# The state's part of a Mamba-2 SSD output: head by head into the output's PSUM bank, with a scaled C, in place of one matmul, a scaled copy and transposes

## The chip, the core and the metric

The kernel runs on one core of one Trainium2 chip. The metric is device time in microseconds (us), the median of several executions. The engines are named as the profile names them: PE is TensorE (PEld its weight loads), DVE is VectorE, ACT is ScalarE, POOL is GpSimd, and SP is SyncE, which issues DMAs here. Each engine runs its own instructions strictly in the order in which they stand, and waits for the others by semaphores. POOL also issues some of the DMAs, from the same queue of instructions in which its arithmetic stands.

## The reference

The kernel computes one hybrid decoder layer on 528 tokens (16 meta tokens and 512 real ones, width 1024): a Mamba-2 SSD branch and a forgetting-attention branch, gated and merged. The change is in the SSD branch. It has 32 heads of 64 channels in 4 groups of 8 heads, a state of 128 per channel, and chunks of 128 tokens. What matters of the reference:

```python
xdt = (xh * dt[..., None]).reshape(Bsz, nc, CHUNK, G, R, P)
a_cs = jnp.cumsum(adt, axis=-1)
seg = a_cs[..., :, None] - a_cs[..., None, :]
decay = jnp.exp(jnp.where(causal, seg, -jnp.inf))
cb = jnp.einsum("bclgn,bcsgn->bcgls", cm, bm)
y_diag = jnp.einsum("bcgls,bcgrls,bcsgrp->bclgrp", cb, decay, xdt)
...
def step(h, inp):
    s, d = inp
    return h * d[..., None, None] + s, h
_, h_in = lax.scan(step, h0, (states, chunk_decay))
y_off = jnp.einsum("bclgn,bcgrpn,bcgrl->bclgrp", cm, h_in, jnp.exp(a_cs))
return (y_diag + y_off).reshape(Bsz, Lp, H, P)
```

`y_off` is the state's part: C of a token times the state at the chunk's start, scaled by the decay since then, which differs for each head and token.

## The kernel before

The work is one long list of projections (the helper `gemm`, line 106: 128-wide weight columns against all tokens, in three products of split halves, `uhi`/`ulo` against `whi`/`wlo`) with the two branches' own work between them. The program is written group by group; a scheduler with a timeline of its own then sets the order of the instructions on each engine, so that projections stand between the pieces of the SSD work. A weight tile comes by DMA (`raw`), ACT rounds it (line 90, `whi`) and DVE takes the rest (line 91, `wlo`). A projection's PSUM tile `mm` has 2 buffers, so a projection can start when the one before the last has been copied out (lines 380, 411, 691 on ACT, line 693 on DVE).

The SSD core (`ssd_core`, below) goes over 4 groups, and in a group over 5 chunks: chunk 0 holds the meta tokens, chunks 1 to 4 have 128 tokens each and an output. I call what chunk c from 1 to 4 does for the output block c. For a block before the change:

- A DMA from POOL's queue (line 449) brings the cumulated log decay of 8 heads, repeated over 128 partitions, into `ab`, one of 4 buffers `big`.
- DVE subtracts a column for each head (line 451, 8 instructions, in place), ACT takes the exponential of the tile (line 453), DVE multiplies by the masked C·B (line 454).
- PE transposes the chunk's x into `px` (line 440); DVE scales it to `xdt` (line 443) and `xdd` (line 446). PE makes the chunk's own state from `xdd` (line 466, into `pst`).
- The state's part: PE multiplies C with the state `h` (line 456, tokens on partitions, into `py`), ACT scales each head's 64 columns by its decay (line 460, 8 instructions, into `y`), and PE transposes the four 128-column pieces of `y` into the output's PSUM tile `pt` (line 477).
- The chunk's own part: 8 matmuls of 64 weight columns, one a head, add into `pt` (line 481). The heads of even number write partitions 0 to 63, the others 64 to 127.
- DVE adds `pt` to the skip (line 486). POOL decays the state (line 471) and DVE adds `pst` (line 472); `h` has 2 buffers.

All PSUM tiles but `mm` come from one pool `ax` of 4 banks. Buffers of a name are used in turn, so in the kernel before the transfer of a block takes the buffer of the same block of the group before.

Of the kernel before, what the change touches and what calls it, by code (L numbers as in the profile page):

```python
# [37 lines left out]
def hybrid_kernel(ctx, tc, x, meta, norm_pre, w_in, conv_w, conv_b, dt_bias, a_log, d_skip,  # L38
# [25 lines left out]
    def big4(shape=(P, 1024)):  # L64
        return st("big4", list(shape), BUFS["big4"])
# [4 lines left out]
    def ax_ps():  # L70
        return axp.tile([P, 512], F32, tag="ax", name=nm("ax"))

    V, S, PE, GP = nc.vector, nc.scalar, nc.tensor, nc.gpsimd
    HE, UE, SE, YS_ACT = GP, V, V, True
# [297 lines left out]
    eac = cst.tile([P, 5, 32], F32, name="eac")  # L372
    S.activation(eac, ac_t, AF.Exp)
# [19 lines left out]
    def heads(ap):  # L393
        return ap.rearrange("p (h x) -> p h x", h=HG)
# [21 lines left out]
    def ssd_core(g, bt, ct, xs, zs):  # L416
# [18 lines left out]
        for c in range(5):  # L435
# [11 lines left out]
            if c:  # L447
                ab = big4((P, HG, P))
                nc.gpsimd.dma_start(out=ab, in_=acs_d[hs, a:b].partition_broadcast(P))
                for i in range(HG):  # L450
                    V.tensor_scalar(ab[:, i], ab[:, i], ac_t[:, c, g * HG + i:g * HG + i + 1], 0.0,  # L451
                                    op0=ALU.subtract, op1=ALU.min)
                S.activation(ab, ab, AF.Exp)  # L453
                V.tensor_mul(ab, ab, cbt[:, c - 1].unsqueeze(1).broadcast_to([P, HG, P]))
                py = ax_ps()
                PE.matmul(py, ct[:, a:b], h, start=True, stop=True)  # L456
                y = row("tmp", (P, T))
                if YS_ACT:
                    for i in range(HG):
                        S.activation(y[:, i * 64:(i + 1) * 64], py[:, i * 64:(i + 1) * 64], AF.Copy,  # L460
                                     scale=eac[:, c, g * HG + i:g * HG + i + 1])
                else:
                    V.tensor_mul(heads(y), heads(py), hb(eac[:, c, hs]))
# [10 lines left out]
            if c:  # L474
                pt = ax_ps()
                for j in range(4):
                    PE.matmul(pt[:, j * P:(j + 1) * P], y[:, j * P:(j + 1) * P], ident,  # L477
                              is_transpose=True, start=j == 0, stop=False)
                for i in range(HG):
                    r = (i % 2) * 64  # L480
                    PE.matmul(pt[r:r + 64, (i // 2) * P:(i // 2 + 1) * P],  # L481
                              xdt[:, i * 64:(i + 1) * 64], ab[:, i], start=False,
                              stop=i >= HG - 2)
# [362 lines left out]
```

## Time and profile before

| | before |
|---|---|
| median of 3 runs | 853.15 us (852.42 to 853.45) |
| the profiled execution | 853.14 us, span of its instructions 851.4 us |
| PE busy | 834.7 us, 98% of the span |
| DVE, ACT, POOL busy | 601.8, 442.5, 72.1 us |
| TensorE's granted clock, mean | 0.998 |

The profiled execution took 853.14 us and the profile covers 851.4 us of it, from the first instruction to the end of the last; 1.7 us lie around the span. Its time is the median's within 0.01 us, so a sum made against it can be read against the median as it is. Matmuls overlap their neighbours in the pipeline, so the time that one costs on PE is read from the chain of waits, which cuts the overlaps away, and not from its own duration.

### The profile page before, as it was taken

The numbers are of one execution on the slowest core, as the hardware profiler recorded it, in microseconds if no ns is written. First come the engines' busy times: TensorE is split into PE (matmuls) and PEld (weight loads), VectorE is DVE, ScalarE is ACT, GpSimd is POOL, SyncE is SP. The second block draws the span as 40 slices with busy tenths as digits, with TensorE's granted clock in tenths as the row PEclk, the third lists the DMA queues.
The fourth block names the chain that finished last, engine by engine and source line by source line (L and its number), as shares of the span: only waits on it lengthen the run. The fifth ranks groups of instructions, "written<-read, shape, count | busy, mean of one in ns | idle before, by whom it ended". The sixth has DMA issues, their size and how long they took to land.

```text
span 851.4 us, 13318 instructions
## 1 busy us (share of the span) xinstructions
PE 834.7 (98%) x5037; PEld 722.9 (85%) x5037; DVE 601.8 (71%) x1296; ACT 442.5 (52%) x906; POOL 72.1 (8%) x136
## 2 busy tenths in 40 slices
PE   6999999999999999999999999999999999999996
PEld 4998889778987799778898988888888898888885
DVE  7799598946994689746786766666767666647735
ACT  6455455445543366333574666566666666522332
POOL 3031110011000100011100001000000100000000
PEclk9999999999999999999999999999999999999999
DMA  7245344235332453222322222222322222224422
GB/s 214 76 127 162 78 110 112 77 96 115 89 96 79 96 123 99 88 62 51 86 91 76 75 75 76 75 76 75 77 75 76 76 75 75 75 84 166 146 75 99
DMA packets 114500, 79.94 MB, mean 94 GB/s; under 512 B 5684, under 2 KB 108260, under 8 KB 114436
## 3 DMA queue, kind: packets, MB, share of 16 engines
q1 hardware_dynamic: 110692, 70.08, 28.9%
q0 software_dynamic: 3744, 9.01, 5.2%
q8 instruction: 39, 0.64, 0.3%
q14 instruction: 25, 0.20, 0.1%
HBM read 76.65 MB, written 2.44 MB: 93 GB/s over the span
## 4 chain that ended last, share of the span: by engine, by line
PE 90%; DMA 3%; DVE 3%; issue 2%; ACT 0%; POOL 0%; SPq 0%; DVEq 0%; POOLq 0%
PE mm L106 71%; PE ax L657 3%; PE mm L781 3%; PE ax L631 2%; DMA big<-acs_d 2%; PE ax L781 1%; PE ax L481 1%; PE ax L596 1%; PE ax L466 1%; PE ax L595 1%; PE ax L456 1%; PE ax L440 1%; DMA big<-in_x_dram 1%; DVE big L451 1%; PE ax L477 1%
## 5 line engine op out<-in xcount | busy, mean ns | idle before, releaser
L106 PE MATMUL mm<-ulo,whi 128*128 128x264 f32 (+1 forms) x1024 | 286.5, 328 | 0.0
L106 PE MATMUL mm<-uhi,whi 128*128 128x264 f32 (+1 forms) x1024 | 284.5, 327 | 0.0
L90 ACT CAST whi<-raw 128x1024 fp32r<-128x1024 f32 x118 | 124.2, 1052 | 143.4 <-PE mm L106 115.4
L91 DVE TENSOR_TENSOR wlo<-raw,whi 128x1024 fp32r<-128x1024 f32 x117 | 142.8, 1220 | 68.4 <-ACT whi L90 31.5
L106 PE MATMUL mm<-uhi,wlo 128*128 128x264 f32 (+1 forms) x1024 | 189.4, 326 | 0.0
L106 PEld LDWEIGHTS mm<-uhi,whi 128*128 128x128 f32 x1024 | 172.3, 188 | 16.9 <-issue 2.7
L106 PEld LDWEIGHTS mm<-ulo,whi 128*128 128x128 f32 x1024 | 172.4, 188 | 16.3 <-issue 2.9
L106 PEld LDWEIGHTS mm<-uhi,wlo 128*128 128x128 f32 x1024 | 152.6, 188 | 14.5 <-issue 0.7
L106 PE MATMUL mm<-yhi,whi 128*128 128x512 f32 x192 | 78.6, 409 | 0.7 <-ACT ms L691 0.7
L106 PE MATMUL mm<-ylo,whi 128*128 128x512 f32 x192 | 76.6, 399 | 0.0
L601 ACT ACTIVATE tmp<-tmp,nmx 128x400 f32<-128x400 f32 (+4 forms) x80 | 41.2, 517 | 28.1 <-DVE nmx L598 26.0
L384 DVE SCALAR_TENSOR_TENSOR xbc<-xp,hcol,xbc 128x528 f32<-128x528 f32 x72 | 54.1, 763 | 0.5 <-ACT tmp L387 0.3
L106 PE MATMUL mm<-yhi,wlo 128*128 128x512 f32 x192 | 54.1, 401 | 0.0
L598 DVE CUSTOM_DVE_ANT_0 tmp<-ax,maskf 128x288 f32<-128x288 f32 (+4 forms) x80 | 32.7, 434 | 23.3 <-PE ax L596 23.0
L451 DVE TENSOR_SCALAR big<-big,dtok 128x128 f32<-128x128 f32 x128 | 28.8, 289 | 27.2 <-DMA big<-acs_d 27.2
L460 ACT ACTIVATE tmp<-ax,eac 128x64 f32<-128x64 f32 x128 | 28.2, 330 | 34.8 <-PE ax L456 34.8
L106 PEld LDWEIGHTS mm<-yhi,whi 128*128 128x128 f32 x192 | 36.1, 188 | 10.7 <-issue 2.3
L106 PEld LDWEIGHTS mm<-ylo,whi 128*128 128x128 f32 x192 | 36.1, 188 | 9.5 <-issue 2.6
L106 PEld LDWEIGHTS mm<-yhi,wlo 128*128 128x128 f32 x192 | 35.8, 188 | 9.2 <-issue 2.2
L657 PE MATMUL ax<-big,vt 128*128 128x512 f32 (+2 forms) x144 | 35.4, 329 | 0.0
L453 ACT ACTIVATE big<-big 128x1024 f32<-128x1024 f32 x16 | 17.0, 1061 | 33.9 <-DVE big L451 33.9
L693 DVE TENSOR_TENSOR ms<-ms,mm 128x512 f32<-128x512 f32 x24 | 16.5, 686 | 23.3 <-PE mm L106 23.3
(258 smaller groups left out, 1167.3 us busy)
## 6 DMA issues: line engine op xcount, KB each, us to landing
raw<-in_w_in_dram SPq DMA_DIRECT2D x88, 512.0 KB, 3.8
big<-acs_d POOLq DMA_DIRECT2D x16, 512.0 KB, 6.2
raw<-in_w_proj_ssd_dram SPq DMA_DIRECT2D x16, 512.0 KB, 3.4
raw<-in_w_proj_att_dram SPq DMA_DIRECT2D x8, 512.0 KB, 3.4
raw<-in_w_out_dram SPq DMA_DIRECT2D x8, 512.0 KB, 3.5
big<-in_x_dram SPq DMA_DIRECT2D x4, 512.0 KB, 6.5
yhi<-in_x_dram SPq DMA_DIRECT2D x2, 1024.0 KB, 6.9
out_dram<-big SPq DMA_DIRECT2D x3, 512.0 KB, 2.6
```

Source lines behind the costliest of these rows:

```text
L90: S.copy(hi, raw)
L91: (GP if nparts[0] <= 1 else V).tensor_sub(lo, raw, hi.bitcast(F32))
L106: PE.matmul(o, lw, u[:, a:b], start=i == 0, stop=i == len(seq) - 1)
L384: V.scalar_tensor_tensor(o, xp[:, k:k + L], cw[:, 24 * k + ct:24 * k + ct + 1], o, op0=ALU.mult, op1=ALU.add)
L451: V.tensor_scalar(ab[:, i], ab[:, i], ac_t[:, c, g * HG + i:g * HG + i + 1], 0.0, op0=ALU.subtract, op1=ALU.min)
L453: S.activation(ab, ab, AF.Exp)
L460: S.activation(y[:, i * 64:(i + 1) * 64], py[:, i * 64:(i + 1) * 64], AF.Copy, scale=eac[:, c, g * HG + i:g * HG + i + 1])
L598: V.tensor_tensor_reduce(pr[i][:, a:b], o, m, -1.0, 3e38, ALU.add, ALU.min, nmx[:, n:n + 1])
L601: S.activation(pr[i][:, a:b], pr[i][:, a:b], AF.Exp, bias=nmx[:, i:i + 1], scale=-1.0, accum_out=rsum[:, n:n + 1])
L631: PE.transpose(dest[b, i], pr[i][:, s0:s0 + P], ident)
L657: PE.matmul(po[:, o:T], w, q, start=i == 0, stop=i == len(seq) - 1)
L781: PE.matmul(pss[s][t], a, b, start=kq == 0 and i == 0, stop=kq == 3 and i == len(seq) - 1)
```

## The change

The matmul of line 456, the eight scalings of line 460, the tile `eac` of decays and the four transposes of line 477 go. In their place ACT writes the exponential of the whole transferred tile into a second `big` buffer, `eb`, and POOL multiplies it, head by head the same, with C of the chunk. Then 8 more matmuls of 64 weight columns, with the old state `ho` as weights and `eb` as the moving tile, write the output's PSUM tile ahead of the 8 that were there. The exponential reads `ab` before DVE changes `ab` in place.

```diff
--- before.py
+++ after.py
@@ -71,7 +71,7 @@
         return axp.tile([P, 512], F32, tag="ax", name=nm("ax"))
 
     V, S, PE, GP = nc.vector, nc.scalar, nc.tensor, nc.gpsimd
-    HE, UE, SE, YS_ACT = GP, V, V, True
+    HE, UE, SE = GP, V, V
 
     def raised(n=1):
         return tc.high_priority(offset=n * 1000000)
@@ -369,8 +369,6 @@
     V.tensor_mul(dtd, dtd, dt_t)
     dch = cst.tile([P, 5, 32], F32, name="dch")
     S.activation(dch, lastv, AF.Exp)
-    eac = cst.tile([P, 5, 32], F32, name="eac")
-    S.activation(eac, ac_t, AF.Exp)
 
 
     def conv(ps, ct, o):
@@ -445,22 +443,16 @@
                 xdd = row("tmp", (P, T))
                 V.tensor_mul(heads(xdd[0:n]), heads(px[0:n]), hb(dtd[0:n, c, hs]))
             if c:
-                ab = big4((P, HG, P))
+                ab, eb = big4((P, HG, P)), big4((P, HG, P))
                 nc.gpsimd.dma_start(out=ab, in_=acs_d[hs, a:b].partition_broadcast(P))
+                S.activation(eb, ab, AF.Exp)
+                GP.tensor_mul(eb, eb, ct[:, a:b].unsqueeze(1).broadcast_to([P, HG, P]))
                 for i in range(HG):
                     V.tensor_scalar(ab[:, i], ab[:, i], ac_t[:, c, g * HG + i:g * HG + i + 1], 0.0,
                                     op0=ALU.subtract, op1=ALU.min)
                 S.activation(ab, ab, AF.Exp)
                 V.tensor_mul(ab, ab, cbt[:, c - 1].unsqueeze(1).broadcast_to([P, HG, P]))
-                py = ax_ps()
-                PE.matmul(py, ct[:, a:b], h, start=True, stop=True)
-                y = row("tmp", (P, T))
-                if YS_ACT:
-                    for i in range(HG):
-                        S.activation(y[:, i * 64:(i + 1) * 64], py[:, i * 64:(i + 1) * 64], AF.Copy,
-                                     scale=eac[:, c, g * HG + i:g * HG + i + 1])
-                else:
-                    V.tensor_mul(heads(y), heads(py), hb(eac[:, c, hs]))
+                ho = h
             if c < 4:
                 pst = ax_ps()
                 PE.matmul(pst, btok[0:n, c], xdd[0:n], start=True, stop=True)
@@ -473,14 +465,12 @@
                 h = h2
             if c:
                 pt = ax_ps()
-                for j in range(4):
-                    PE.matmul(pt[:, j * P:(j + 1) * P], y[:, j * P:(j + 1) * P], ident,
-                              is_transpose=True, start=j == 0, stop=False)
-                for i in range(HG):
-                    r = (i % 2) * 64
-                    PE.matmul(pt[r:r + 64, (i // 2) * P:(i // 2 + 1) * P],
-                              xdt[:, i * 64:(i + 1) * 64], ab[:, i], start=False,
-                              stop=i >= HG - 2)
+                for q, (w, m) in enumerate(((ho, eb), (xdt, ab))):
+                    for i in range(HG):
+                        r = (i % 2) * 64
+                        PE.matmul(pt[r:r + 64, (i // 2) * P:(i // 2 + 1) * P],
+                                  w[:, i * 64:(i + 1) * 64], m[:, i], start=q == 0 and i < 2,
+                                  stop=q == 1 and i >= HG - 2)
                 o = (c - 1) * P
                 for j in range(4):
                     V.scalar_tensor_tensor(
```

Lines of the changed kernel are 2 lower than before up to the transfer (447), and the others follow so: exponential of `eb` 448, POOL's multiplication 449, subtraction 451, exponential 453, multiplication 454 (these three as before), `px` 438, `xdt` 441, `xdd` 444, `pst` 458, the state on POOL 463 and on DVE 464, all 16 head matmuls 471, the skip 476, evacuations 378 and 683. Numbers behind a name tell buffers apart. Four `big` buffers now serve two blocks in place of four: block 3 takes those of block 1, block 4 those of block 2, and the next group's block 1 those of block 3.

The first place is POOL's queue in the third group. Before, its transfers (`big_535` and on) are for the fourth group's blocks:

```order
L471 TENSOR_TENSOR h_2804<-h_2768,dch 128x512
L471 TENSOR_TENSOR h_2858<-h_2804,dch 128x512
L449 DMA big_535_3740<-acs_d 128x8x128
L471 TENSOR_TENSOR h_2912<-h_2858,dch 128x512
L449 DMA big_544_3794<-acs_d 128x8x128
L449 DMA big_553_3848<-acs_d 128x8x128
L449 DMA big_561_3900<-acs_d 128x8x128
```

In the changed kernel, `big_407` and `big_414` are blocks 3 and 4 of the third group itself, and `big_408` and `big_415` are their `eb`:

```order
L463 TENSOR_TENSOR h_2762<-h_2734,dch 128x512
L447 DMA big_407_2845<-acs_d 128x8x128
L463 TENSOR_TENSOR h_2812<-h_2762,dch 128x512
L449 TENSOR_TENSOR big_408_2846<-big_408_2846,xbc_2177 128x1024
L447 DMA big_414_2893<-acs_d 128x8x128
L463 TENSOR_TENSOR h_2862<-h_2812,dch 128x512
L449 TENSOR_TENSOR big_415_2894<-big_415_2894,xbc_2177 128x1024
L447 DMA big_523_3690<-acs_d 128x8x128
```

The transfer of block 4 now stands behind the multiplication of block 3, and both are of the group that is being computed.

The second place is DVE in the third group, around its second block. Before, the subtractions there (`big_535`) are for the fourth group; `h_2858` is the third group's state:

```order
L693 TENSOR_TENSOR ms_2172<-ms_2172,mm_3123 128x512
L451 TENSOR_SCALAR big_535_3740<-big_535_3740,dtok 128x128 x3
L91 TENSOR_TENSOR wlo_3175<-raw_3173,whi_3174 128x1024
L451 TENSOR_SCALAR big_535_3740<-big_535_3740,dtok 128x128 x5
L472 TENSOR_TENSOR h_2858<-h_2858,ax_2856 128x512
L486 SCALAR_TENSOR_TENSOR xbc_2342<-xbc_2342,dcol,ax_2861 128x128
L486 SCALAR_TENSOR_TENSOR xbc_2408<-xbc_2408,dcol,ax_2861 128x128
L486 SCALAR_TENSOR_TENSOR xbc_2474<-xbc_2474,dcol,ax_2861 128x128
L486 SCALAR_TENSOR_TENSOR xbc_2540<-xbc_2540,dcol,ax_2861 128x128
L443 TENSOR_TENSOR tmp_2883<-ax_2878,dtok 128x512
L446 TENSOR_TENSOR tmp_2885<-ax_2878,dtd 128x512
```

In the changed kernel the subtractions are those of block 3 (`big_407`), `ms` are evacuations of projections, `h_2812` is the state that block 3 multiplies, and `tmp_2843` is block 3's `xdd`:

```order
L683 TENSOR_TENSOR ms_2123<-ms_2123,mm_3059 128x512
L451 TENSOR_SCALAR big_407_2845<-big_407_2845,dtok 128x128 x8
L683 TENSOR_TENSOR ms_2138<-ms_2138,mm_3073 128x512
L91 TENSOR_TENSOR wlo_3125<-raw_3123,whi_3124 128x1024
L464 TENSOR_TENSOR h_2812<-h_2812,ax_2810 128x512
L454 TENSOR_TENSOR big_407_2845<-big_407_2845,tmp_2718 128x1024
L476 SCALAR_TENSOR_TENSOR xbc_2308<-xbc_2308,dcol,ax_2815 128x128
L476 SCALAR_TENSOR_TENSOR xbc_2374<-xbc_2374,dcol,ax_2815 128x128
L476 SCALAR_TENSOR_TENSOR xbc_2440<-xbc_2440,dcol,ax_2815 128x128
L476 SCALAR_TENSOR_TENSOR xbc_2506<-xbc_2506,dcol,ax_2815 128x128
L441 TENSOR_TENSOR tmp_2841<-ax_2836,dtok 128x512
L444 TENSOR_TENSOR tmp_2843<-ax_2836,dtd 128x512
```

The evacuation, the weight's rest, the state, the skip of block 2 and block 3's `xdd` now stand behind block 3's own subtractions and multiplication. On PE, between the head matmuls of block 2 and of block 3, stand there the 4 transposes of `px`, 24 projections of 512 columns and the matmul of line 458 that needs `xdd`; between block 3 and block 4's first 8 stand 4 transposes and 12 projections of 264 columns, then 15 such between block 4's first and last 8.

The third place is ACT at the end of the first group. Before (`big_264`, `big_273` are blocks 2 and 3 of the second group, `mm_1446` is a projection beside the first group's last blocks):

```order
L453 ACTIVATE big_264_1864<-big_264_1864 128x1024
L460 ACTIVATE tmp_1159<-ax_1157,eac 128x64 x8
L90 CAST whi_1573<-raw_1572 128x1024
L453 ACTIVATE big_273_1918<-big_273_1918 128x1024
L380 COPY xp_1495<-mm_1446 128x528
L381 ACTIVATE xbc_1439<-xp_1495,hcol 128x528
```

In the changed kernel (`big_251` and `big_259` are blocks 1 and 2 of the second group, with `big_252` and `big_260` their `eb`; `mm_1428` is the projection beside the first group's fourth block):

```order
L448 ACTIVATE big_252_1793<-big_251_1792 128x1024
L90 CAST whi_1555<-raw_1554 128x1024
L453 ACTIVATE big_251_1792<-big_251_1792 128x1024
L448 ACTIVATE big_260_1843<-big_259_1842 128x1024
L378 COPY xp_1477<-mm_1428 128x528
L379 ACTIVATE xbc_1421<-xp_1477,hcol 128x528
```

The evacuation of `mm_1428` now stands behind an exponential that waits for the transfer of the second group's block 2. On PE, the projection that takes over the PSUM buffer of `mm_1428` starts 50 projection matmuls of 264 columns after the first group's last head matmul.

## Rows read from the trace of the kernel before

**Rows 1.** The page: engines, granted clock by slices, the chain that ended last.

```profile
span 851.4 us, 13318 instructions
...
PE 834.7 (98%) x5037; PEld 722.9 (85%) x5037; DVE 601.8 (71%) x1296; ACT 442.5 (52%) x906; POOL 72.1 (8%) x136
...
PEclk9999999999999999999999999999999999999999
...
PE 90%; DMA 3%; DVE 3%; issue 2%; ACT 0%; POOL 0%; SPq 0%; DVEq 0%; POOLq 0%
```

**Rows 2.** Who waited for whom, TensorE: total us, times, longest us.

```profile
PE ax L456 <- DVE h L472: 1.8, 3, 0.7
...
PE mm L106 <- ACT ms L691: 0.7, 1, 0.7
PE ax L466 <- DVE tmp L446: 0.3, 1, 0.3
```

**Rows 3.** The chain in order of time, second group: start us, us, what.

```profile
173.60 0.86 PE ax L456 x2
...
176.23 2.77 PE mm L106 x12
...
179.12 0.44 PE ax L440 x4
179.55 0.33 PE ax L477 x3
179.88 1.05 PE ax L481 x16
180.93 0.30 issue
...
191.16 5.45 DMA big<-acs_d
...
198.29 1.14 DVE wlo L91
199.43 0.61 DVE h L472
...
200.08 1.12 PE ax L456 x2
201.20 3.02 PE mm L106 x25
```

**Rows 4.** VectorE in order of time, second group: start us, us, instruction, idle before.

```profile
196.63 1.66 DVE L451 TENSOR_SCALAR big<-big,dtok 128x128 f32<-128x128 f32 x8 [4.32 <-DMA big<-acs_d]
```

**Rows 5.** VectorE in order of time, first group.

```profile
108.68 1.29 DVE L451 TENSOR_SCALAR big<-big,dtok 128x128 f32<-128x128 f32 x2
109.89 0.76 DVE L384 SCALAR_TENSOR_TENSOR xbc<-xp,hcol,xbc 128x528 f32<-128x528 f32 x1
```

**Rows 6.** GpSimd in order of time, the same stretch.

```profile
108.85 1.03 POOL L471 TENSOR_TENSOR h<-h,dch 128x512 f32<-128x512 f32 x1 [6.46 <-DVE h L472]
```

**Rows 7.** Line 451, all its instructions: nanoseconds min/median/max, first and last start.

```profile
L451 DVE TENSOR_SCALAR big<-big,dtok x128: 264/281/1099, 64.2 to 313.6; 128x128 f32<-128x128 f32 x128
```

**Rows 8.** Groups by line and form: busy us, mean ns, idle before us, GpSimd.

```profile
L471 POOL TENSOR_TENSOR h<-h,dch 128x512 f32<-128x512 f32 x12 | 12.5, 1039 | 155.5 <-ACT h L469 102.0 <-DVE h L472 53.5
...
L91 POOL TENSOR_TENSOR wlo<-raw,whi 128x1024 fp32r<-128x1024 f32 x1 | 2.4, 2363 | 1.4 <-ACT whi L90 1.4
```

**Rows 9.** The same view, ScalarE.

```profile
L90 ACT CAST whi<-raw 128x1024 fp32r<-128x1024 f32 x118 | 124.2, 1052 | 143.4 <-PE mm L106 115.4 <-issue 11.9 <-PE mm L781 6.3
L460 ACT ACTIVATE tmp<-ax,eac 128x64 f32<-128x64 f32 x128 | 28.2, 330 | 34.8 <-PE ax L456 34.8
...
L453 ACT ACTIVATE big<-big 128x1024 f32<-128x1024 f32 x16 | 17.0, 1061 | 33.9 <-DVE big L451 33.9
...
L380 ACT COPY xp<-mm 128x528 f32<-128x528 f32 x24 | 14.3, 596 | 14.4 <-DVE xbc L384 9.2 <-PE mm L106 4.8 <-issue 0.3
...
L493 ACT ACTIVATE tmp<-xbc 128x512 f32<-128x512 f32 x4 | 2.5, 633 | 2.3 <-DVE xbc L491 2.3
```

**Rows 10.** The chain in order of time, first group.

```profile
101.43 6.23 DMA big<-acs_d
...
109.97 0.68 DVE xbc L384
...
111.44 0.60 DVE tmp L443
112.03 0.61 DVE tmp L446
```

**Rows 11.** VectorE in order of time, second group, after its second block.

```profile
190.00 1.12 DVE L486 SCALAR_TENSOR_TENSOR xbc<-xbc,dcol,ax 128x128 f32<-128x128 f32 x4
```

**Rows 12.** DMA issues: KB each, median us to landing.

```profile
big<-acs_d POOLq DMA_DIRECT2D x16, 512.0 KB, 6.2
```

## The prediction

> **What bounds the kernel now.** I read the page first. PE is busy for 834.7 of 851.4 us, at full clock in every slice, and makes 90% of the chain that ended last [rows 1]; DVE and ACT have room. So a change is worth what it takes from PE's own work, plus or minus the time that PE stands and waits. PE's waits come next: in the SSD part they are small, 1.8 us for the state of line 472 and 0.3 us for `xdd` [rows 2]; the 0.7 us for `ms` I leave as it is. Then I read the chain in the second group, which shows what stands behind such a wait. At 191.16 a transfer into `big` starts; it is meant for the next group and nobody needs it. DVE waits for it 4.32 us at line 451 [rows 4], then does line 91 and only then the state, and PE's matmul of line 456 waits for that state [rows 3]. A wait of DVE on a transfer reaches PE through what is queued behind it. That is the place to look at in the changed kernel, where the transfer is for a block that is needed at once.
>
> **PE's own work.** Durations are those of the chain [rows 3]. Each of the 16 blocks loses the matmul of line 456 (0.86 us) and four transposes (0.33 for three, 0.44 for four): 1.30, in all 20.8 us. It gains 8 head matmuls like those of line 481, 1.05 us. Of that I put about 0.10 down to the last pair's tail, which vanishes where the next 8 follow at once, as in 12 of the 16 blocks: 12 x 0.95 + 4 x 1.05 = 15.6 us. The bounds are 16.8 (all at 1.05) and 13.8 (0.86, the same multiplications as in line 456). I take 15.6: PE's work falls by **5.2 us** (4.0 to 7.0). The old waits of 2.1 us are counted as gone, because I count all waits anew.
>
> **What costs nothing.** ACT loses 8 x 0.33 us a block and gains one exponential of 1.06 [rows 9]; it is busy 52%, and its order is counted below. One exponential (`eac`) at the start lies beside projections. DVE's work is unchanged. In blocks 1 and 2 the `big` tiles are loaded long before PE comes; the projections of a whole group cover them, and without these their chain of some 10 us would show.
>
> **The new waits.** Block 3 takes block 1's buffers, so its transfer can start only when PE has done block 1. I follow the third group, with 0 at the end of block 1; a hand-over between engines takes 0.05 (199.43 + 0.61 to 200.08, [rows 3]).
>
> 1. The transfer is issued 0.30 later and lands after 5.45 [rows 3]: 5.75. ACT's exponential for `eb` takes 1.06 [rows 9]: 6.85.
> 2. Now POOL's multiplication and DVE's subtractions are released by the same event. POOL's 512-wide multiplication takes 1.04 [rows 8]; twice that is 2.08, to 9.0 (the nearest other row, a 1024-wide subtraction, has 2.36). The subtractions take 1.66 [rows 4], but not beside POOL: at 108.85 POOL began its 1.03 us, and the second of two subtractions, which began beside it, ended with it (the pair took 1.29, [rows 5, 6]; the longest of line 451 is 1099 ns where the median is 281, [rows 7]). So I let one go first, POOL's whole instruction next, and seven (1.45) after it: 10.5.
> 3. DVE then does what the order puts behind them: evacuation 0.60 (priced as 111.44, [rows 10]), line 91 1.14, the state 0.61 [rows 3], the multiplication by C·B 1.14 (the form of line 91; ACT's exponential before it ends by 11.6), the skip of block 2 1.1 [rows 11], `xdt` 0.60 and `xdd` 0.61 [rows 10]: 5.8 us, to 16.3.
> 4. PE: transposes 0.44, 24 projections at 2.77/12 = 0.231, line 458's matmul 0.86, block 2 at 2.0, again 0.44 and 24 x 0.231: it stands before block 3's `xdd` matmul at 14.8. **It waits 1.5 us.** Block 3 is done at 16.35 + 0.86 + 2.0 = 19.2.
> 5. Block 4's transfer stands behind the multiplication on POOL: issued at 9.05, landed 14.5, exponential 15.6, POOL's multiplication to 17.75, subtractions held up by it to 19.45, then evacuation, line 91 and state: 21.8. PE arrives at 19.2 + 0.44 + 12 x 0.121 (3.02/25) = 21.1. **It waits 0.7.**
>
> So the third and the fourth group wait 2.2 us each. In the second group the evacuation is ACT's and one step fewer stands on DVE, but only 6 projections stand ahead of block 4: PE waits 0.85 before block 3 (0.15 of it for a PSUM buffer whose copy stands behind ACT's second exponential) and 1.45 before block 4. In the first group POOL's state update stands ahead of the transfer (0.3), transfers take 6.2 (6.23 in [rows 10]), and DVE has two convolution steps of 0.68 more in its queue: 2.3 and 2.15.
>
> At a group's end the order on ACT counts. The transfer of the next group's block 2 starts with the end of block 4 and lands after 0.3 + 6.2 (the median, [rows 12]); with the exponential, 7.6 us after that end. In the first group the copy of a projection stands right behind (0.60, [rows 9]): 8.2, and PE needs its buffer after 50 x 0.121 = 6.05: 2.15 us. In the second group a cast, two squares and a copy follow (1.05 + 2 x 0.63 + 0.60), ending at 10.5, and PE is there after 73 x 0.121 = 8.8: 1.7. In the third, one square and the copy end at 8.85 against 69 x 0.121 = 8.35: 0.5.
>
> First group 6.6, second 4.0, third 2.7, fourth 2.2: **15.5 us**.
>
> The sum: 853.1 - 5.2 - 2.1 + 15.5 = **861.3 us**; the profiled execution has the median's time.
>
> [...]
>
> **The rivals.**
> - *POOL and DVE do not hold each other up.* Against it stands the one case of [rows 5, 6], for it that it is one. Then step 2 ends at 8.55 and step 3 at 14.35, before PE comes, and step 5's state at 19.65, when PE comes. The third and fourth group wait 0.1 together besides the 0.5 at the end, the second 0.2 + 1.7, the first 0.35 + 1.95 + 2.15: 6.95 us in all, and 852.7 us, no change that can be measured.
> - *Faster: the transfers all take the short time, and POOL and DVE don't clash.* With 5.45 [rows 3] in place of 6.2, the waits at the groups' ends shrink by 0.75, 0.75 and 0.5, and the first group's by 0.35 and 1.5: 3.1 us remain, 848.9. The change wins where new waits are under 7.3 - 1.7 = 5.6 us. For it: transfers of both lengths stand in the trace; against it: the median of all 16 is 6.2 [rows 12]. With no wait at all it would be 845.8.
> - *The long durations everywhere.* Transfers of 6.23 [rows 10] and 2.36 for the multiplication [rows 8] make 4.3 us in the third and in the fourth group, 6.1 in the second, 7.25 in the first, with 0.5: 22.5, and 868.3 us.
>
> **How the numbers follow.** I give the forecast 0.50 (some 856 to 865, the range of PE's work and of a few hand-overs), the first rival 0.20, the faster one 0.15, the long one 0.15. About 0.2% (1.7 us) is what a measurement of this kernel can tell from no change, so 851.4 to 854.9 is the same: nearly all of the first rival, 0.17. Slower are the forecast, the long case and the rest of the first rival: 0.68. Faster: 0.15. A range of 850 to 867 leaves out most of the faster case and the top of the long one, about 0.2 together.
>
> **What the profile after will show.** The head matmuls of line 471 at about 2.0 us for 16. POOL's multiplication at 2.08. In every group, line 451 of blocks 3 and 4 at over 3 us for its eight, with one of about 2 us; if none exceeds 0.3, the first rival holds. PE waiting at line 458 for `xdd` and at line 471 for the state in each group, and at a projection for an ACT copy after the first and second group, in all 12 to 19 us. A lower granted clock in these waits, of which this trace shows nothing, would make it slower than the sum; so would a place in the order that I have not followed. An arrival of PE later than I count would make it faster.

## The result: slower, and the profile after

The changed kernel takes 865.4 us (median of 4, 862.9 to 867.9) against 852.8 us before on the same chip: a ratio of 1.0145, 95% interval 1.0132 to 1.0158. The forecast was 861.3 us. The profiled execution took 867.9 us, with a span of 866.2 and a mean granted clock of 0.989; the two executions at 0.997 took 862.9 and 863.9, the two at 0.989 and 0.991 took 867.9 and 866.9. So some 4 us of a long execution go with the clock; at 0.997, near the clock of before, the change still costs some 10.6 us.

The page of the changed kernel, busy times and the shares of the chain by engine, against [rows 1]:

```profile
PE 837.4 (97%) x5197; PEld 727.5 (84%) x5197; DVE 629.2 (73%) x1296; ACT 429.2 (50%) x793; POOL 116.2 (13%) x152
...
PE 82%; DVE 8%; issue 4%; DMA 4%; ACT 1%; POOL 0%; SPq 0%; DVEq 0%; ACTq 0%; POOLq 0%
```

DVE gains 27 us though it was given no work. Groups by line of the changed kernel, DVE and POOL (busy us and mean ns, then the idle time before):

```profile
L382 DVE SCALAR_TENSOR_TENSOR xbc<-xp,hcol,xbc 128x528 f32<-128x528 f32 x72 | 61.2, 863 | 1.1 <-ACT xbc L379 0.9
L451 DVE TENSOR_SCALAR big<-big,dtok 128x128 f32<-128x128 f32 x128 | 42.4, 416 | 16.7 <-ACT big L448 16.7
...
L449 POOL TENSOR_TENSOR big<-big,xbc 128x1024 f32<-128x1024 f32 x16 | 41.2, 2583 | 43.2 <-ACT big L448 27.0 <-DVE xbc L386 16.2
```

Lines 451 and 382 do what they did before. All instructions of line 451 (min, median, max ns), and the group of line 382 in the kernel before, where it is line 384:

```profile
L451 DVE TENSOR_SCALAR big<-big,dtok x128: 267/276/2501, 69.4 to 405.2; 128x128 f32<-128x128 f32 x128
...
L384 DVE SCALAR_TENSOR_TENSOR xbc<-xp,hcol,xbc 128x528 f32<-128x528 f32 x72 | 54.1, 763 | 0.5 <-ACT tmp L387 0.3
```

Line 451's median is 276 ns (281 before [rows 7]), but the longest went from 1099 [rows 7] to 2501; the mean of line 382 went from 763 to 863. The waits of PE, without those of the start (6.7 us before, 6.9 after); they answer to [rows 2]:

```profile
PE ax L458 <- DVE tmp L444: 7.1, 4, 2.5
...
PE mm L106 <- DVE z L410: 4.1, 2, 2.4
...
PE ax L471 <- DVE h L464: 1.7, 1, 1.7
...
PEld ax L471 <- POOL big L449: 1.5, 1, 1.5
...
PE mm L106 <- ACT ms L681: 1.0, 2, 0.7
...
PE ax L438 <- DVE xbc L386: 0.9, 1, 0.9
```

New are 7.1 us for `xdd` (line 458), 4.1 for `z` (a projection's evacuation that stands on DVE behind the convolution's steps), 0.9 for `xbc` (such a step itself) and 1.7 for the state, against 1.8 for it before. The weight loads (PEld) also wait 1.5 us for POOL, once; PE itself was busy with line 458's second matmul then, so this is no time of PE's. The chain, one row of the first group and then the third group, in order of time (start, us, what), which answers to [rows 3]:

```profile
99.08 1.92 PE ax L471 x32
...
284.94 0.35 PE ax L471 x6
...
285.69 6.07 DMA big<-acs_d
...
291.84 1.07 ACT big L448
...
292.93 0.05 DVE big L451
292.98 0.90 issue
...
293.90 1.45 issue
295.35 1.72 DVE big L451 x7
297.08 0.59 DVE ms L683
297.67 1.14 DVE wlo L91
298.81 0.60 DVE h L464
299.41 1.13 DVE big L454
...
302.10 0.69 DVE tmp L444
...
302.92 1.10 PE ax L458 x2
304.02 3.53 PE ax L471 x32
```

What releases the transfer ends at 285.29. That is not block 1's end: PE's timeline and POOL's there show the last 8 of the block's 16 head matmuls, the transfer and POOL's multiplication:

```profile
285.10 1.04 PE L471 MATMUL ax<-big,tmp 128*64 128x128 f32 x16
...
285.69 0.92 POOL L447 DMA_DIRECT2D big<-acs_d  x1 [6.61 <-PE ax L471]
...
292.98 2.37 POOL L449 TENSOR_TENSOR big<-big,xbc 128x1024 f32<-128x1024 f32 x1 [5.29 <-ACT big L448]
```

The transfer waits for the first 8, which end at 285.26 (284.17 + 1.09), and leaves 0.45 us before the last 8 end at 286.14. So the buffer that it fills is one that the last 8 don't read: block 3's `ab` takes the buffer of block 1's `eb`, not of its `ab`. The transfer lands, ACT's exponential ends, and DVE does 0.05 us of a subtraction. Then comes "issue" for 0.90 and 1.45 us, in which DVE waits for nothing that a semaphore shows. POOL's multiplication runs from 292.98 for 2.37 us, and DVE goes on at 295.35, when it ends. Behind it stands DVE's queue of 5.7 us down to `xdd` at 302.79, and PE's line 458, which waits. So steps 1 to 4 are to be seen one behind the other. The same holds for blocks prepared ahead. The timeline of DVE and of POOL, ahead of the first group (start, us):

```profile
63.14 0.75 DVE L382 SCALAR_TENSOR_TENSOR xbc<-xp,hcol,xbc 128x528 f32<-128x528 f32 x1
...
66.53 2.90 DVE L382 SCALAR_TENSOR_TENSOR xbc<-xp,hcol,xbc 128x528 f32<-128x528 f32 x1
69.36 3.78 DVE L451 TENSOR_SCALAR big<-big,dtok 128x128 f32<-128x128 f32 x8
...
65.62 3.25 POOL L449 TENSOR_TENSOR big<-big,xbc 128x1024 f32<-128x1024 f32 x1
69.15 2.54 POOL L449 TENSOR_TENSOR big<-big,xbc 128x1024 f32<-128x1024 f32 x1 [0.28 <-ACT big L448]
```

A step of the convolution (line 382) takes 0.75 us alone and 2.90 beside POOL's multiplication. Not every DVE instruction is held. In the third group `xdd` (line 444), which reads PSUM, runs inside POOL's next multiplication and takes its usual time (0.67, and 0.68 at 287.83 with no multiplication beside it), as does the evacuation behind it (line 683, 0.67):

```profile
302.10 0.67 DVE L444 TENSOR_TENSOR tmp<-ax,dtd 128x512 f32<-128x512 f32 x1
...
301.87 2.35 POOL L449 TENSOR_TENSOR big<-big,xbc 128x1024 f32<-128x1024 f32 x1 [0.42 <-ACT big L448]
```

Last the granted clock: the third figure from the right is PEclk, 1.00 in a stretch without a wait, then a stretch behind the first wait for `z` and one behind the wait for `xdd` in the third group:

```profile
core 0: us, PE busy (x) PEld busy (x) DVE busy (x) ACT busy (x) POOL busy (x), PEclk, DMA share, GB/s
68.00:72.00 4.00, 4.00 (x23) 3.46 (x22) 4.00 (x4) 2.11 (x2) 3.41 (x2) 1.00 0.00 0
75.50:78.90 3.40, 3.12 (x8) 2.50 (x9) 3.40 (x11) 1.48 (x2) 0.21 (x1) 0.54 0.59 159
304.20:307.60 3.40, 3.40 (x33) 3.15 (x32) 3.40 (x11) 1.06 (x1) 0.94 (x2) 0.54 0.00 0
```

119.90 to 123.30, 164.20 to 167.60 and 403.20 to 406.60, behind the second wait for `z` and those for `xdd` in the first and fourth group, show 0.54, 0.53 and 0.54. The 3.0 us from 75.50, 119.90, 164.20, 304.00 and 403.20 on show 0.50 each; in the kernel before, all five stretches show 1.00. The stretch in the third group holds the head matmuls of the third group's block 3: 3.53 us in the chain above, where the first group's at 99.08 took 1.92.

### The profile page after: what moved, and what is told of

Its sections match the earlier page's. It is cut to its first block, busy times and chain, and to the rows that moved or that the text cites. A ratio compares the mean times of both kernels' runs of the same rounds, so it can differ in the third digit from the quotient of the medians.

```text
span 866.2 us, 13561 instructions
## 1 busy us (share of the span) xinstructions
PE 837.4 (97%) x5197; PEld 727.5 (84%) x5197; DVE 629.2 (73%) x1296; ACT 429.2 (50%) x793; POOL 116.2 (13%) x152
## 4 chain that ended last, share of the span: by engine, by line
PE 82%; DVE 8%; issue 4%; DMA 4%; ACT 1%; POOL 0%; SPq 0%; DVEq 0%; ACTq 0%; POOLq 0%
PE mm L106 65%; DMA big<-acs_d 3%; PE ax L647 3%; PE mm L771 3%; PE ax L471 2%; PE ax L621 2%; DVE big L451 1%; PE ax L771 1%; PE ax L586 1%; PE ax L585 1%; PE ax L458 1%; DVE xbc L382 1%; DMA big<-in_x_dram 1%; DVE xbc L386 1%; PE ax L438 1%
## 5 line engine op out<-in xcount | busy, mean ns | idle before, releaser
L106 PE MATMUL mm<-yhi,whi 128*128 128x512 f32 x192 | 76.4, 398 | 1.0 <-ACT ms L681 1.0
L382 DVE SCALAR_TENSOR_TENSOR xbc<-xp,hcol,xbc 128x528 f32<-128x528 f32 x72 | 61.2, 863 | 1.1 <-ACT xbc L379 0.9
L591 ACT ACTIVATE tmp<-tmp,nmx 128x240 f32<-128x240 f32 (+4 forms) x80 | 41.2, 517 | 29.0 <-DVE nmx L588 25.5
L451 DVE TENSOR_SCALAR big<-big,dtok 128x128 f32<-128x128 f32 x128 | 42.4, 416 | 16.7 <-ACT big L448 16.7
L106 PE MATMUL mm<-yhi,wlo 128*128 128x512 f32 x192 | 51.6, 390 | 0.0
L588 DVE CUSTOM_DVE_ANT_0 tmp<-ax,maskf 128x144 f32<-128x144 f32 (+4 forms) x80 | 32.8, 434 | 23.0 <-PE ax L586 22.7
L449 POOL TENSOR_TENSOR big<-big,xbc 128x1024 f32<-128x1024 f32 x16 | 41.2, 2583 | 43.2 <-ACT big L448 27.0
L448 ACT ACTIVATE big<-big 128x1024 f32<-128x1024 f32 x16 | 16.9, 1057 | 53.7 <-DMA big<-acs_d 52.9
L453 ACT ACTIVATE big<-big 128x1024 f32<-128x1024 f32 x16 | 16.9, 1059 | 31.9 <-DVE big L451 31.9
```

The costliest lines, as they stand in the source:

```text
L106: PE.matmul(o, lw, u[:, a:b], start=i == 0, stop=i == len(seq) - 1)
L382: V.scalar_tensor_tensor(o, xp[:, k:k + L], cw[:, 24 * k + ct:24 * k + ct + 1], o, op0=ALU.mult, op1=ALU.add)
L449: GP.tensor_mul(eb, eb, ct[:, a:b].unsqueeze(1).broadcast_to([P, HG, P]))
L588: V.tensor_tensor_reduce(pr[i][:, a:b], o, m, -1.0, 3e38, ALU.add, ALU.min, nmx[:, n:n + 1])
L591: S.activation(pr[i][:, a:b], pr[i][:, a:b], AF.Exp, bias=nmx[:, i:i + 1], scale=-1.0, accum_out=rsum[:, n:n + 1])
```

## Experiments

My theory after the trace is that POOL's multiplication holds DVE, and DVE's queue carries it to PE. Rivals: the late transfers alone make the waits (A), the holds alone make them and lateness costs nothing (B), PE waits for `eb` itself (C), the loss comes through POOL's queue, in which transfers stand behind multiplications (D). All ratios are to the kernel before, timed beside.

| kernel | median us | ratio (95% interval) |
|---|---|---|
| multiplication on DVE | 847.9 | 0.9939 (0.9927 to 0.9951) |
| no decay in the state's part | 847.6 | 0.9935 (0.9923 to 0.9947) |
| no multiplication | 844.8 | 0.9904 (0.9890 to 0.9919) |
| before, two buffers a block | 852.9 | 0.9999 (0.9990 to 1.0007) |
| before, unused multiplication | 862.1 | 1.0109 (1.0092 to 1.0126) |
| before, unused exponential | 849.7 | 0.9968 (0.9955 to 0.9980) |
| POOL in 8 pieces | 862.5 | 1.0112 (1.0097 to 1.0128) |
| POOL with one input | 850.2 | 0.9967 (0.9956 to 0.9979) |
| transfers from SP | 884.6 | 1.0367 (1.0351 to 1.0383) |
| POOL for blocks 1, 2 | 852.8 | 0.9999 (0.9990 to 1.0007) |
| POOL for blocks 3, 4 | 861.8 | 1.0107 (1.0092 to 1.0122) |
| multiplication on DVE, written late | 846.4 | 0.9929 (0.9916 to 0.9943) |

**The multiplication on DVE.**

```diff
-                GP.tensor_mul(eb, eb, ct[:, a:b].unsqueeze(1).broadcast_to([P, HG, P]))
+                V.tensor_mul(eb, eb, ct[:, a:b].unsqueeze(1).broadcast_to([P, HG, P]))
```

> The multiplication of `eb` by C goes from POOL to DVE; buffers, transfers and exponentials stay. Theory (POOL's multiplication holds DVE, on top of transfers that start late): the holds go (some 2 us at each wait for `xdd`, and those of the convolution), 1.2 us of DVE's own work comes in for a block; the waits fall from 16.7 us to some 6, and the time to about 854. Rival A (the late transfers alone make the waits, POOL and DVE hardly hold each other): DVE's queue gets longer by 1.2 us at each of the waits, and the time rises to 868 to 872.

It took 847.9, under my 854: faster than the kernel before, and 17.5 under the changed one. PE's waits and DVE's line 449 in its trace:

```profile
PE mm L106 <- DVE ylo L508: 1.0, 1, 1.0
PE ax L458 <- DVE tmp L444: 0.9, 1, 0.9
...
PE mm L106 <- DVE z L410: 0.5, 1, 0.5
...
L449 DVE TENSOR_TENSOR big<-big,xbc 128x1024 f32<-128x1024 f32 x16 | 19.2, 1218 | 11.2 <-ACT big L448 11.2
```

DVE does in 1.22 us what POOL does in 2.58, and the longest subtraction (line 451) takes 717 ns in place of 2501. Rival A falls: DVE's queue got longer, the transfers stayed late, and the waits went.

**Without the decay, and without the multiplication.** Both leave out part of the computation, as their expectations say.

```diff
-                ab, eb = big4((P, HG, P)), big4((P, HG, P))
+                ab = big4((P, HG, P))
+                eb = ct[:, a:b].unsqueeze(1).broadcast_to([P, HG, P])
...
-                S.activation(eb, ab, AF.Exp)
-                GP.tensor_mul(eb, eb, ct[:, a:b].unsqueeze(1).broadcast_to([P, HG, P]))
```

> Leaves out the decay of the state's part: the 8 added head matmuls take C itself as their moving tile, so there is no `eb`, no second exponential, no multiplication, and a block takes one `big` buffer again. What is left is the change of PE's own work. By the prediction's term (5.2 us less) some 848; by the head matmuls in the trace after (1.9 us for 16, against 0.86 + 0.44 + 1.05 before, 0.45 less in each of 16 blocks, 7.2) some 846. Both theories say the same; a time near 853 or above would mean that PE's work was not reduced and both are wrong.

The second removes only the last of these lines.

> Leaves out the multiplication by C alone: `eb` is the exponential, written by ACT into the second buffer as in the change. Two blocks still share four buffers, so transfers still start late. Theory (holds matter most): 848 to 852, waits of under 5 us in all, line 451 of block 3 at 1.7 us for eight, no wait at the convolution. Rival A (late transfers alone): 860 or more, with line 458's waits of about 2 us in each group. Rival B (the holds alone, late transfers cost nothing): 846.

They took 847.6 and 844.8. The first has a span of 844.9 us, 6.5 under the kernel before, with about the same waits (2.9 us, 2.2 of them for the state). The second is the sharper test: transfers late, exponential there, and with POOL's multiplication alone taken away the time falls by 20.6 us. Of PE's waits behind the start 0.7 us for `ms` are left in it, and this:

```profile
PE ax L470 <- DVE h L463: 0.8, 2, 0.6
```

That is rival B's number (846), not the 848 to 852 of mine, which still gave the late transfers a share. So late transfers alone cost nothing that can be seen here.

**The kernel before with two buffers a block.**

```diff
-                ab = big4((P, HG, P))
+                ab, spare = big4((P, HG, P)), big4((P, HG, P))
```

> The kernel before, with a second `big` buffer taken for each block and not used: the transfers of blocks 3 and 4 start as late as in the changed kernel, and nothing else differs. Theory: by the prediction's steps the transfer (5.75), the subtractions (1.66) and DVE's queue (5.8) end at 13.2, ahead of PE at 14.8: 853 to 855. Rival A: waits of about 2 us in each group, 858 to 862. Rival B: 853.

852.9, no difference, but this tests nothing: the transfers did not start late. The four of the first group leave together, first in the kernel before, then in this run:

```profile
56.48 3.58 POOL L449 DMA_DIRECT2D big<-acs_d  x4 [0.58 <-PE ax L356]
...
56.02 3.58 POOL L449 DMA_DIRECT2D big<-acs_d  x4 [0.58 <-PE ax L356]
```

The third group's leave from 180.84 on, where the kernel before has 181.23, a whole group ahead. A tile that no instruction writes held no buffer back. What late transfers alone cost is read from the kernel without the multiplication: block 3's in its third group leaves at 269.82, while block 1's last head matmuls run (269.23 to 270.27).

**The preparation in the kernel before, unused.** The multiplication first, then its control without the multiplication.

```diff
-                ab = big4((P, HG, P))
+                ab, eb = big4((P, HG, P)), big4((P, HG, P))
                 nc.gpsimd.dma_start(out=ab, in_=acs_d[hs, a:b].partition_broadcast(P))
+                S.activation(eb, ab, AF.Exp)
+                GP.tensor_mul(eb, eb, ct[:, a:b].unsqueeze(1).broadcast_to([P, HG, P]))
```

> The kernel before, with the change's preparation added and not used: a second `big` buffer, ACT's exponential into it, POOL's multiplication by C. No matmul reads it, so nobody can wait for `eb`. Theory (POOL's multiplication holds DVE's instructions, and DVE's queue carries it to PE): the same holds as in the changed kernel, so about as much on top of before as the multiplication cost there (865.4 against 844.8 without it, 20.6): 866 to 874. Rival C (PE waits for `eb` itself, which POOL finishes late): 853 to 856.

> The kernel before with the second buffer and ACT's exponential into it, not used, and without POOL's multiplication: the control for the unused multiplication. Theory: ACT has room, late transfers cost nothing, 852.5 to 854. If it is near 862, the exponential and not the multiplication made that loss.

862.1 and 849.7: a multiplication that nobody reads costs 12.4 us, so C is not needed for most of the loss. It is less than I expected, because the holds are not the same: nobody reads `eb`, so its buffer comes free early, and the transfers are not late. In this order `xdd` (line 446 there) stands ahead of the subtractions (line 453) on DVE, and PE never waits for it. Its waits are those at the convolution (5.5 for `z`, 1.2 for `xbc`). Block 4's transfer on POOL and DVE's timeline, in the third group:

```profile
253.78 0.92 POOL L449 DMA_DIRECT2D big<-acs_d  x1 [0.42 <-POOL xp L378]
...
285.72 0.68 DVE L446 TENSOR_TENSOR tmp<-ax,dtd 128x512 f32<-128x512 f32 x1
...
287.35 3.11 DVE L453 TENSOR_SCALAR big<-big,dtok 128x128 f32<-128x128 f32 x8
```

The eight subtractions of block 4 are held here too, 3.11 us in place of 1.66, but PE's need stands in front of them, and the transfer had left 33 us ahead of them (8 us in the changed kernel). So D has no part in these 12.4 us either, and of the theories the hold is left for them. What the multiplication costs beyond them in the changed kernel I put down to blocks 3 and 4, which are late there; that is argued and was not tested. The control came out 3 us below the kernel before. Its trace has none of the 1.8 and 0.3 us waits of [rows 2], but 1.8 us of others at the start (line 250), so its waits don't explain it; PE is busy 831.7 us in it in place of 834.7, and why is not shown. I take some 3 us as what a change of the order alone can make between such kernels, an estimate from this one run.

**POOL's multiplication in 8 pieces.**

```diff
-                GP.tensor_mul(eb, eb, ct[:, a:b].unsqueeze(1).broadcast_to([P, HG, P]))
+                for i in range(HG):
+                    GP.tensor_mul(eb[:, i], eb[:, i], ct[:, a:b])
```

> POOL's multiplication in 8 instructions of 128 columns, one a head, in place of one of 1024; all else as in the change. If DVE is held for one whole POOL instruction at a time, a piece of some 0.32 us (2.58 / 8) holds one DVE instruction and DVE gets in between: the longest L451 falls from 2.5 to under 0.8 us, the convolution steps lose under 0.4 each, and the time is 850 to 858. If POOL's whole work passes first however it is cut, the time stays at 863 to 868.

862.5, above my 850 to 858. POOL's pieces and DVE's subtractions (line 452 there; min, median, max ns):

```profile
L450 POOL TENSOR_TENSOR big<-big,xbc 128x128 f32<-128x128 f32 x128 | 74.7, 619 | 45.7 <-ACT big L448 30.3 <-DVE xbc L386 15.4
...
L452 DVE TENSOR_SCALAR big<-big,dtok x128: 268/492/956, 67.1 to 400.7; 128x128 f32<-128x128 f32 x128
```

The longest subtraction falls to 956 ns, and the waits at the convolution are down to 0.3. But a piece takes 619 ns in the mean (459 in the median, 445 at the least), not 320. The eight of a block take 3.37 us beside the third group's subtractions and 6.4 beside the first convolution (12.75 for two blocks), in the mean 4.67 (74.7 / 16). Block 4's transfer stands behind them, and PE waits 8.4 us for the state. Cut up, POOL's work takes longer than the 2.58 of one piece; whether DVE or a cost of each instruction makes it so was not separated, since even the shortest piece is longer than 320 ns.

**One input on POOL.**

```diff
-                GP.tensor_mul(eb, eb, ct[:, a:b].unsqueeze(1).broadcast_to([P, HG, P]))
+                GP.tensor_scalar(eb, eb, 0.5, 2.0, op0=ALU.mult, op1=ALU.mult)
```

> POOL's two-input multiplication becomes a one-input instruction (times 0.5, times 2) on the same tile: leaves out the factor C. Theory: DVE is held for as long as POOL's instruction lasts, whatever POOL does; by its duration (unknown; between 1.0, as the 512-wide state, and 2.58) the time stands between 844.8 and 865.4: some 850 at 1.1 us, 858 at 1.8. If only two-input instructions of POOL hold DVE, it is 845 at any duration, and L451 keeps its median of 0.29 us at the longest too.

850.2, with POOL's median at 1133 ns, where I expected some 850 for 1.1. A one-input instruction holds DVE as well, and the longest subtraction (1081) is about as long as POOL's instruction, where the kernel without any multiplication there has 623 at most. Line 449 and line 451 (min, median, max ns):

```profile
L449 POOL TENSOR_SCALAR big<-big x16: 1040/1133/3491, 65.2 to 385.3; 128x1024 f32<-128x1024 f32 x16
...
L451 DVE TENSOR_SCALAR big<-big,dtok x128: 267/275/1081, 67.6 to 387.5; 128x128 f32<-128x128 f32 x128
```

**Transfers from SP.**

```diff
-                nc.gpsimd.dma_start(out=ab, in_=acs_d[hs, a:b].partition_broadcast(P))
+                nc.sync.dma_start(out=ab, in_=acs_d[hs, a:b].partition_broadcast(P))
```

> The changed kernel with the transfers issued from SP's queue in place of POOL's, so that block 4's transfer no longer stands behind POOL's multiplication (step 5 of the prediction). Theory (holds): DVE is held as before, 861 to 866; only block 4's transfer starts some 2.5 us earlier. Rival D (the loss comes through POOL's queue, in which the transfers wait for multiplications): 845 to 852. Transfers that wait for a buffer can now hold up weight loads behind them on SP, which would show as PE waits for `raw` tiles' products and add to the time.

884.6, outside every expectation, and it does not test D. SP's queue in the third group:

```profile
301.62 0.37 SPq L89 DMA_DIRECT2D raw<-in_w_in_dram  x1
302.08 0.54 SPq L447 DMA_DIRECT2D big<-acs_d  x1
```

Block 4's transfer stands behind a weight load that waits until line 91 on DVE has freed its buffer, and that line stands behind block 3's held subtractions (they end at 299.86, line 91 runs from 300.38). It leaves at 302.08, 6.05 us after POOL's multiplication for block 3 began (296.03); in the changed kernel this was 2.31 (292.98 to 295.29). Then block 4's own subtractions wait for it, and the state behind them: 16.0 us of PE's waits, up to 5.5 each. D is bounded by the trace after instead: where nothing on POOL stands ahead of it, a transfer leaves 0.4 to 0.7 us behind the first 8 head matmuls that it waits for. Block 2's end at 294.08 in the third group and at 107.89 in the first, and POOL's multiplication kept block 4's transfer until 295.29 and 110.44. So it came some 0.5 to 2 us later for that, and what this costs PE in blocks 3 and 4 was not measured apart.

**POOL for some of the blocks.** Blocks 1 and 2 first; the second run has `V` and `GP` exchanged.

```diff
-                GP.tensor_mul(eb, eb, ct[:, a:b].unsqueeze(1).broadcast_to([P, HG, P]))
+                (GP if c < 3 else V).tensor_mul(eb, eb, ct[:, a:b].unsqueeze(1).broadcast_to([P, HG, P]))
```

> POOL multiplies for blocks 1 and 2 of a group, which are prepared ahead, and DVE for blocks 3 and 4. By the prediction's step that costs the prefetched blocks at nothing: the time of the variant with all of it on DVE, 847.9. By the theory after the trace (POOL's multiplication holds the convolution's steps for the next group's x, and PE waits for `z` and `xbc` behind them: 5.0 us of waits, and stretches of a lower granted clock behind them): 854 to 858, near the 9.1 that the unused preparation cost the kernel before.

> The reverse: DVE multiplies for blocks 1 and 2, POOL for blocks 3 and 4, which share the buffers of blocks 1 and 2 and come late. By the prediction (all of the loss stands here): 863 to 865. By the theory after the trace (waits at line 458 of 7.1, for the state 1.7, and the clock behind them): 857 to 861; with the run above it should add up to the 17.5 between 847.9 and 865.4.

852.8 and 861.8, the one a little under and the other a little over what the theory after the trace gave: against 847.9 with none on POOL, blocks 1 and 2 cost 4.9 us and blocks 3 and 4 cost 13.9, together 18.8 where 17.5 was to be split. PE's waits in the first of them are 2.6 us for `z` and `xbc` (5.0 in the changed kernel), 1.5 for line 502 (the output's scaling, behind the convolution on DVE), and 1.1 for `xdd`. That is 2.8 us more than with none on POOL (2.4), so some 2 of the 4.9 are no waits. The two for the convolution:

```profile
PE mm L106 <- DVE z L410: 1.7, 1, 1.7
...
PE ax L438 <- DVE xbc L386: 0.9, 1, 0.9
```

In the other PE waits 5.1 us for `xdd` and 7.2 for the state.

**The multiplication on DVE, written late.**

```diff
-                GP.tensor_mul(eb, eb, ct[:, a:b].unsqueeze(1).broadcast_to([P, HG, P]))
...
             if c:
+                V.tensor_mul(eb, eb, ct[:, a:b].unsqueeze(1).broadcast_to([P, HG, P]))
                 pt = ax_ps()
```

> The multiplication on DVE, written behind the state update, just ahead of the head matmuls, so that where the order follows the program the subtractions and the state go first. Theory: the waits of the variant with the multiplication on DVE (2.4 us, 0.9 of them for `xdd`) fall a little: 846 to 848. If the order hardly moves, 847.9 as there.

846.4, the fastest version that computes the reference, 0.7% under the kernel before. Its interval overlaps with that of the first variant; that it is better than that one is not shown.

## Why the prediction was right or wrong

The sign and the mechanism held, and 865.4 lies in the range. Step by step:

- **PE's own work, 5.2 us less (4.0 to 7.0).** About right, on the low side. In the trace 16 head matmuls take 1.92 in place of 1.05, 0.87 more where I took 0.95; split ones take 2 x 1.02. So 20.8 - 12 x 0.87 - 4 x 0.99 = 6.4. By spans, the kernel without multiplication is 8.5 us under the one before (851.4 - 842.9), of which 1.3 are fewer waits: 7.2; the one without decay gives 6.5. With the 3 us that I allow for the order alone, 5 to 7 is what I can say.
- **Steps 1 to 4, the hold before block 3.** Right, but for its premise that the transfer can start only when PE has done block 1: it left 0.45 us before that end (286.14), where I had 0.30 behind it, and then took 6.07, where I had 5.45, so it landed at 5.6 (forecast 5.75). The two errors cancel, which is luck. From that end: exponential done at 6.8 (6.85), POOL done at 9.2 (9.0), subtractions done at 10.9 (10.5), `xdd` at 16.7 (16.3), PE there at 14.9 (14.8), a wait of 1.9 us (1.5). The median of all 16 transfers fell from 6.2 [rows 12] to 5.9. POOL took 2.37, the upper bound of the prediction, where I took 2.08. In the four groups PE waits 7.1 us at line 458; the forecast has 2.3 + 0.85 + 1.5 + 1.5 = 6.15.
- **Step 5, block 4's state, 5.0 us in all.** Too large: 1.7, once, in the second group. In the third group the state was ready at 21.9 (308.00), as forecast (21.8), but PE came at 23.4 (309.50) and not at 21.1: it took 3.53 us for block 3's head matmuls, at the lower clock (0.54 from 304.20 to 307.60), in place of 1.92, and some of the rest it had lost at line 458.
- **ACT's copies at a group's end, 4.35 us.** Wrong: none appeared; the wait for `ms` went from 0.7 to 1.0. The same premise failed: I let the transfer for the next group's block 2 start with the end of block 4. In the first group it left at 126.28, behind block 4's first 8 head matmuls (125.73) and ahead of the last 8 (128.51 to 129.60). So the exponential was done by 133.07, 3.5 us after the block's end and not 7.6, and the copy began at 132.98.
- **"In blocks 1 and 2 the tiles are loaded long before PE comes."** This step failed too, and it is the one that the experiments tested. It is true of the tiles, and I priced them at nothing for it. But POOL's multiplications for them hold the convolution's steps (2.90 us in place of 0.75 for one of line 382; ahead of the first group the subtractions as well), on which the next projections wait: 5.0 us of waits in the trace (4.1 for `z`, 0.9 for `xbc`), and 4.9 us of time by the experiment, of which about 2.8 are waits. I had followed the hold only to the subtractions of blocks 3 and 4.
- **The clock.** Named as what could make it worse, and not in the sum. 1.1% of 866.2 less 0.2% of 851.4 is 7.8 us at most, by estimate, since part of it falls on waits; executions at 0.997 and at 0.989 to 0.991 lie about 4 us apart.

The sum with what was measured: -7.2 (PE) - 2.1 (old waits) + 14.1 (7.1 + 4.1 + 0.9 + 1.7, and 0.3 more for `ms`) + 4 to 7.8 (clock) = 8.8 to 12.6 us, against 14.8 in the profiled spans. So 2 to 6 us are not assigned. They are not waits: PE's idle time grew by 12.1 us (866.2 - 837.4 less 851.4 - 834.7), which the waits in this sum give (14.1 - 2.1). They lie in PE's busy time, 837.4 us against 827.5 without the multiplication, where the lower clock lies too. That the forecast's waits (15.5) and the measured ones are near each other is luck in the parts: 4.35 that did not come, and 3.3 of 5.0 for the state, stand against 5.0 that I had not seen.

Beside POOL's multiplication the longest subtraction of line 451 took 2.50 us (median 0.28), and a step of line 382 took 2.90 in place of 0.75. For the multiplication itself the trace has 2.35 at the least, 2.45 in the median and 2.58 in the mean, where I took 2.08. Nearer was a row of the kernel before that I had only as an upper bound, a two-input subtraction of the same width on POOL at 2.36 [rows 8].

The first rival (no hold) is refuted, and with it the faster one, which needed it too. The long one (868.3) had POOL's 2.36 right and the transfers too long. With the multiplication off POOL the change is what the faster one hoped for: 846.4 to 847.9.

## What to carry to other kernels

Work on POOL did not simply run beside DVE's here. POOL's multiplications (2.35 to 3.25 us) held DVE nearly for their whole length where DVE stood at one of these instructions, whose tensors are all in SBUF: the subtractions of line 451 (up to 2.50 us, median 0.28) and the convolution's steps of lines 382 (2.90 in place of 0.75) and 386 (three in 6.30 at 155.63, beside two multiplications, where one takes 0.69 at 73.07). Lines 444 and 683, which read PSUM, ran beside one in their usual time (0.67 each). So I would price such work as DVE time for every instruction of the first kind in its stretch, and for prefetched work too. What it costs then depends on what stands behind the held instruction in DVE's queue and who waits for that: the same multiplication cost 20.6 us where two blocks of a group are prepared late, and 12.4 where all are prepared ahead and nobody reads it. And 1.2 us of DVE's own time was cheaper than 2.6 of POOL's.

An experiment's edit can change nothing: a buffer that was taken and never used held no transfer back, and the unchanged time said nothing about late transfers. Only the times of the transfers in its trace show that.

## What was not expected of the hardware

- Eight multiplications of 128 x 128 on POOL took 3.37 us beside DVE's subtractions, where one of 128 x 1024 took 2.37 there. Some of POOL's instructions took longer beside DVE's too: two large ones beside the convolution took 5.57 us, where one takes 2.35 at the least, and the state's multiplication (line 463) took 1.95 at 299.50, beside DVE's line 454, in place of 1.04.
- PE's granted clock fell to 0.50 behind five of PE's waits of 1.7 to 2.6 us, and head matmuls that take 1.92 us took 3.53 there. Behind a sixth wait, of 1.7 us for the state in the second group, it stayed at 1.00, and so it did behind the 5.7 us at the start of the kernel before, which has no other wait over 0.8 us and no such fall.
